# Hybrid attention block: the negated maximum of the softmax kept as a running minimum in the logits' reduction

## The chip, the cores and the metric

The kernel runs on one core of a Trainium2 chip. A core has five engines with queues of their own: TensorE (PE, matrix products), VectorE (DVE, elementwise work and reductions), ScalarE (ACT, functions), GpSimd (POOL) and SyncE (SP, which here issues nearly all DMAs). Each takes its instructions strictly in the order in which they stand in its queue and waits on semaphores for the others. The metric is the device time of one execution in microseconds (us), the median of three runs.

## The reference, cut to what matters

A decoder block over 2048 positions: a mix of sparse attention (8 heads of 64, one shared key and value) and a gated convolution, then cross attention and a feed-forward part. The change lies in the sparse attention. For each block of 128 queries an indexer picks 256 keys per query; the softmax runs over these alone:

```python
score = jnp.where(causal[None], score, -jnp.inf)
_, sel = lax.top_k(score, topk)
...
logits = jnp.einsum('bqhd,bqkd->bqhk', qb, k_sel).astype(jnp.float32) * (HEAD_DIM ** -0.5)
logits = jnp.where(valid[:, :, None, :], logits, -jnp.inf)
p = jax.nn.softmax(logits, axis=-1).astype(v.dtype)
return jnp.einsum('bqhk,bqkd->bqhd', p, v_sel)
```

## The kernel before

The kernel doesn't gather keys. It computes the logits of a block of queries against all keys up to its diagonal and adds a row of `bias` that is 0 for picked keys and -2^100 for the rest. There are 16 blocks. Block b has (b + 1) x 128 keys, cut into pieces of 512 (`cuts`, L794): blocks 0 to 3 have one piece, 4 to 7 two, 8 to 11 three, 12 to 15 four. `bg_attend` (L774) runs blocks 0 to 7 in one stretch and 8 to 15 in another much later; in both, other work is mixed in: projections and the output product on PE, the search for the 256th largest score on DVE and ACT, and a convolution of 31 taps on POOL (L941, a multiply L962 and an addition L963 per tap).

A block has four pairs of heads (hp). For each pair and piece, and each head e of the pair:

- L815, PE: two products give a tile of logits, 128 queries x up to 512 keys, in PSUM.
- L816, DVE: one instruction adds the bias, writes the masked logits to `prob` in SBUF, and puts their largest value into `mx[:, e, pi]`. The trace shows it as two, the reduction and a short read of the accumulator.
- L820 and L821, DVE, once per pair: the maximum over the pieces, then times -0.125, into `nm`. With one piece L823 alone does it.
- L840, ACT: exp(0.125 x logit + nm), in place, up to 1024 keys at a time, with the sum of each row.
- L889, PE: the probabilities are transposed, 128x128 at a time. L317 (ACT) writes the high part `pth`, L318 (DVE) the rest `ptl`; L854 and L855 (PE) multiply both with the values.
- L874 to L878: the output is transposed back, added up and multiplied by 1 / sum (L878, DVE) into `o`.

While a pair is transposed and multiplied, the logits of the next pair are computed ahead (L902 to L925). So DVE works in turn on the ptl of one pair and the logits of the next. The order on each engine's queue is written by a scheduler, which plays the program through with costs of its own: an instruction taken out or put in can move others.

Of the kernel before, what the change touches and what calls it, by code (L numbers as in the profile page):

```python
# [8 lines left out]
F32 = mybir.dt.float32  # L9
# [6 lines left out]
AF = mybir.ActivationFunctionType  # L16
ALU = mybir.AluOpType
AX = mybir.AxisListType
# [3 lines left out]
P = 128  # L22
# [39 lines left out]
def hybrid_block(ctx: ExitStack, tc: tile.TileContext, x, mem, positions, norm_mix_g, w_in, w_heads, w_out,  # L62
# [4 lines left out]
    V, G, S, PE = nc.vector, nc.gpsimd, nc.scalar, nc.tensor  # L67
# [25 lines left out]
    x, mem, out = x[0], mem[0], out[0]  # L93
# [193 lines left out]
    def right(name, bufs=2):  # L287
        return tc.tile_pool(name=name, bufs=bufs, side="right", reuse_waits="tile")
# [4 lines left out]
    def acc(shape, name="ps_acc"):  # L293
        return pp.tile(shape, F32, name=name, tag="acc", bufs=3)
# [479 lines left out]
    def bg_attend(blks, kv, deep, q0=None):  # L774
        with right("aq") as aq, right("at") as ap, right("av") as av:
# [4 lines left out]
            def block(b):  # L780
                if b not in per:
                    n = (b + 1) * P
                    bias = cb2[:, P - b * P:] if b < 2 else None
                    if bias is None:
                        bias = aq.tile([P, nmax], BF16, name="bias", tag="bias", bufs=ATB)
                        nc.sync.dma_start(out=bias[:, :n], in_=bias_d[b, :, :n])
                    qT = q0 if b == 0 else aq.tile([P, NH, P], F32R, name="qT", tag="qT", bufs=ATB)
                    if b:
                        load_r(qT, columns(q_d, slice(0, NH), b * P, P))
                    o = av.tile([P, NH, HD], F32, name="o", tag="o", bufs=ATB)  # L790
                    per[b] = bias, qT, o
                return per[b]

            def cuts(b):  # L794
                n = (b + 1) * P
                return [(p0, min(512, n - p0)) for p0 in range(0, n, 512)]

            def logits(b, hp, st):

                pcs = cuts(b)  # L800
                bias, qT, o = block(b)
                mx = aq.tile([P, 2, 4], F32, name="mx", tag="mx", bufs=4)
                st["nm"] = nm = aq.tile([P, 2], F32, name="nm", tag="nm")
                st["sm"] = aq.tile([P, 2, 4], F32, name="sm", tag="sm")
                st["pr"] = []
                for pi, (p0, w) in enumerate(pcs):
                    if p0 % 1024 == 0:
                        turn[0] += 1
                        st["pr"].append((ap, av)[turn[0] % 2].tile([P, 2, 1024], F32, name="prob", tag="prob",
                                                                   bufs=(PRA if nmax <= 1024 else PRB) // 2))  # L810
                    prob = st["pr"][-1][:, :, p0 % 1024:]
                    for e in range(2):
                        ps = acc([P, 512])
                        for a in range(2):
                            PE.matmul(ps[:, :w], qT[:, hp * 2 + e, :], ks[p0 // 512][:, a, :w], start=a == 0, stop=a == 1)  # L815
                        V.tensor_tensor_reduce(out=prob[:, e, :w], in0=ps[:, :w], in1=bias[:, p0:p0 + w], scale=1.0,  # L816
                                               scalar=-3.0e38, op0=ALU.add, op1=ALU.max, accum_out=mx[:, e, pi:pi + 1])
                        yield w
                if len(pcs) > 1:
                    V.tensor_reduce(out=nm, in_=mx[:, :, :len(pcs)], op=ALU.max, axis=AX.X)  # L820
                    V.tensor_scalar(out=nm, in0=nm, scalar1=-0.125, scalar2=None, op0=ALU.mult)  # L821
                else:
                    V.tensor_scalar(out=nm, in0=mx[:, :, 0], scalar1=-0.125, scalar2=None, op0=ALU.mult)  # L823

            last, turn = [None], [1]
            behind = []
# [6 lines left out]
            def exps(b, st, pi, es):  # L833

                w = min(1024, (b + 1) * P - pi * 1024)
                if w > 0:
                    for e in es:
                        pr = st["pr"][pi][:, e, :w]
                        with tc.issue_after(last[0]) if last[0] else nullcontext():
                            S.activation(out=pr, in_=pr, func=AF.Exp, scale=0.125, bias=st["nm"][:, e:e + 1],  # L840
                                         accum_out=st["sm"][:, e, pi:pi + 1])

            def weigh(b, hp, st):
# [59 lines left out]
            for _ in logits(*todo[0]):  # L903
                pass
            exps(todo[0][0], todo[0][2], 0, [0, 1])
            for cur, nxt in zip(todo, todo[1:] + [None]):
                ahead = logits(*nxt) if nxt else iter(())
# [977 lines left out]
    op = Scope(right("op"))  # L1885
    for half in range(2):
# [90 lines left out]
        op = Scope(right("op"))  # L1977
# [37 lines left out]
```

## Time and profile before

| | us |
|---|---|
| median of 3 runs | 3303.02 (3301.71 to 3306.49) |
| profiled execution | 3300.71, its span 3298.9 |
| PE busy | 3084.7 (94%) |
| DVE busy | 2478.3 (75%) |
| ACT busy | 1817.3 (55%) |
| POOL busy | 1337.0 (41%) |

The span runs from the first to the last instruction that the profiler saw; the execution's own time is a little longer. Busy shares are means over stages with different limits, so below they are taken by stretch. The first stretch of the sparse attention is about 436 to 760 us, the second about 1905 to 2262 us. In rows of the trace a line such as L816 names the line of the kernel, `out<-in` its tiles, and an arrow in brackets behind an idle time the instruction that ended it.

### The profile page before, as it was taken

Reading aid. Unit: us, or ns where it says so; the run is one execution under the profiler, and the core shown is the slowest. Engines: PE = TensorE matmul, PEld = TensorE weight load, DVE = VectorE, ACT = ScalarE, POOL = GpSimd, SP = SyncE. Lnnn points to the kernel's source line nnn. Section 1 sums busy time; section 2 is a strip of 40 time slices with the busy share of each in tenths; the row PEclk is TensorE's granted clock in tenths of the full one; section 3 lists DMA queues with packets and bytes.
Section 4 is the critical chain, followed back from the end, with each engine's and each line's share of the span. In section 5 each row is a group of like instructions: output and inputs, shape, how many; then the busy total and the mean of one; then the engine's idle time right before and its main releaser. Section 6 shows DMA issues by size and latency. Waiting matters only on the chain.

```text
span 3298.9 us, 45169 instructions
## 1 busy us (share of the span) xinstructions
PE 3084.7 (94%) x16162; PEld 2583.8 (78%) x16162; DVE 2478.3 (75%) x4964; ACT 1817.3 (55%) x3276; POOL 1337.0 (41%) x1141
## 2 busy tenths in 40 slices
PE   7987798999999998999999989999999999999998
PEld 5765576887877788788898878888878777777786
DVE  6899999877758688888788889986555766665445
ACT  6456466655458576667677667775443433333212
POOL 2999702999300699900000049991000144442000
PEclk9999899999999999999999989999999999999999
DMA  7452334543365312121222341103363322222432
GB/s 225 140 158 81 120 99 151 169 146 120 117 203 169 136 49 62 52 60 52 78 64 71 120 149 45 39 20 112 122 252 100 102 83 77 77 81 100 145 103 77
DMA packets 341960, 356.60 MB, mean 108 GB/s; under 512 B 21990, under 2 KB 268518, under 8 KB 340454
## 3 DMA queue, kind: packets, MB, share of 16 engines
q1 hardware_dynamic: 339302, 345.08, 32.8%
q0 software_dynamic: 2432, 8.64, 0.8%
q8 instruction: 127, 2.08, 0.3%
q14 instruction: 99, 0.81, 0.1%
HBM read 271.31 MB, written 82.34 MB: 107 GB/s over the span
## 4 chain that ended last, share of the span: by engine, by line
PE 55%; DVE 29%; ACT 9%; issue 5%; DMA 3%; SPq 0%; DVEq 0%; ACTq 0%
PE ps_w L1483 9%; PE ps_acc L277 6%; PE ps_acc L278 6%; PE ps_acc L276 6%; DVE jkc L687 4%; PE ps_s L277 4%; PE ps_s L278 4%; PE ps_s L276 4%; DVE wl L152 3%; PE ps_acc L815 3%; ACT junk L699 3%; DVE xa_cut L1515 2%; PE ps_tr L889 2%; PE ps_o L278 1%; PE ps_o L277 1%
## 5 line engine op out<-in xcount | busy, mean ns | idle before, releaser
L963 POOL TENSOR_TENSOR vt<-pr_c,vt 128x512 f32<-128x512 f32 x480 | 674.9, 1406 | 39.6
L152 DVE TENSOR_TENSOR wl<-raw,wh 128x1024 fp32r<-128x1024 f32 x252 | 335.2, 1331 | 220.8 <-ACT wh L147 216.1
L147 ACT ACTIVATE wh<-raw 128x1024 fp32r<-128x1024 f32 x252 | 264.8, 1051 | 368.9 <-PE ps_acc L278 174.4
L962 POOL TENSOR_SCALAR pr_c<-u,colsB 128x512 f32<-128x512 f32 x480 | 430.7, 897 | 45.1
L276 PE MATMUL ps_acc<-hp,wh 128*128 128x512 f32 x608 | 239.4, 395 | 0.9 <-ACT hp L322 0.7
L277 PE MATMUL ps_acc<-hp,wh 128*128 128x512 f32 x608 | 238.8, 393 | 0.0
L278 PE MATMUL ps_acc<-hp,wl 128*128 128x512 f32 x608 | 238.0, 392 | 0.0
L1256 POOL TENSOR_SCALAR xa<-xa,rs_y 128x1024 f32<-128x1024 f32 x4 | 4.4, 1123 | 498.6 <-DVE rs_y L170 498.6
L840 ACT ACTIVATE prob<-prob,nm 128x1024 f32<-128x1024 f32 (+7 forms) x192 | 172.1, 897 | 54.2 <-DVE nm L821 33.6
L815 PE MATMUL ps_acc<-kst,qT 128*128 128x512 f32 (+3 forms) x624 | 189.2, 395 | 9.7 <-DVE mx L816 5.1
L816 DVE CUSTOM_DVE_ANT_0 prob<-ps_acc,bias 128x512 f32<-128x512 f32 (+3 forms) x304 | 180.6, 615 | 15.1 <-PE ps_acc L815 12.7
L949 POOL DMA_DIRECT2D u<-u_d x16 | 9.3, 583 | 441.4 <-PE ps_tr L1187 228.4
L1458 POOL TENSOR_TENSOR hp_cut<-xb_cut 128x512 f32<-128x512 f32 x10 | 17.2, 1720 | 421.1 <-PE ps_tr L1404 364.6
L278 PE MATMUL ps_acc<-hh,wl 128*128 128x512 f32 (+1 forms) x384 | 157.8, 412 | 25.7 <-DVE wl L152 18.3
L317 ACT ACTIVATE pth<-ps_tr 128x512 fp32r<-128x512 f32 (+1 forms) x224 | 126.7, 574 | 94.5 <-PE ps_tr L889 84.0
L276 PE MATMUL ps_acc<-wh,hidh 128*128 128x256 f32 (+1 forms) x512 | 168.0, 328 | 7.8 <-ACT halo L1331 7.8
L1483 PE MATMUL ps_w<-T,wh 128*128 128x512 f32 x496 | 157.3, 399 | 18.0 <-DVE hp_cut L1494 18.0
L318 DVE TENSOR_TENSOR ptl<-ps_tr,pth 128x512 fp32r<-128x512 f32 (+1 forms) x224 | 145.7, 656 | 35.8 <-ACT pth L317 34.6
L276 PE MATMUL ps_acc<-hh,wh 128*128 128x512 f32 (+1 forms) x384 | 156.9, 415 | 15.6 <-ACT wh L147 14.7
L277 PE MATMUL ps_acc<-wl,hidh 128*128 128x256 f32 (+1 forms) x512 | 167.9, 328 | 0.0
L278 PE MATMUL ps_acc<-wh,hidl 128*128 128x256 f32 (+1 forms) x512 | 167.8, 328 | 0.0
L855 PE MATMUL ps_o<-ptl,vst 128*128 128x256 f32 x544 | 152.4, 302 | 12.2 <-DVE ptl L318 11.1
(481 smaller groups left out, 9894.9 us busy)
## 6 DMA issues: line engine op xcount, KB each, us to landing
raw<-in_w_down_dram SPq DMA_DIRECT2D x44, 512.0 KB
raw<-in_w_up_dram SPq DMA_DIRECT2D x34, 512.0 KB
raw<-in_w_gate_dram SPq DMA_DIRECT2D x34, 512.0 KB
raw<-in_w_out_dram SPq DMA_DIRECT2D x32, 512.0 KB
raw<-in_w_q_cross_dram SPq DMA_DIRECT2D x32, 512.0 KB
raw<-in_w_o_cross_dram SPq DMA_DIRECT2D x32, 512.0 KB
xt<-in_x_dram SPq DMA_DIRECT2D x24, 512.0 KB
raw<-in_w_in_dram SPq DMA_DIRECT2D x24, 512.0 KB
```

Source lines behind the costliest of these rows:

```text
L147: i = S.activation(out=hi, in_=src, func=AF.Copy)
L152: note(S=i, V=V.tensor_sub(out=lo, in0=src, in1=hi.bitcast(F32)))
L276: PE.matmul(ps, ah, bh, start=first, stop=False)
L277: PE.matmul(ps, ah, bl, start=False, stop=False)
L278: return PE.matmul(ps, al, bh, start=False, stop=last).ins
L815: PE.matmul(ps[:, :w], qT[:, hp * 2 + e, :], ks[p0 // 512][:, a, :w], start=a == 0, stop=a == 1)
L816: V.tensor_tensor_reduce(out=prob[:, e, :w], in0=ps[:, :w], in1=bias[:, p0:p0 + w], scale=1.0, scalar=-3.0e38, op0=ALU.add, op1=ALU.max, a ...
L840: S.activation(out=pr, in_=pr, func=AF.Exp, scale=0.125, bias=st["nm"][:, e:e + 1], accum_out=st["sm"][:, e, pi:pi + 1])
L855: PE.matmul(po, v, ptl[:, j - j0, :], start=False, stop=j == nst - 1)
L962: G.tensor_scalar(out=pr, in0=u[:, i:i + 512], scalar1=cb_w(i, c), scalar2=0.0, op0=ALU.mult, op1=ALU.add)
L963: G.tensor_add(out=vt[:, c, :], in0=pr, in1=vt[:, c, :])
L1483: PE.matmul(ps, x[:, k], y[:, k], start=first and k == i == 0, stop=k == 3 and i == 2, skip_group_check=True)
```

## The change

The reduction of L816 now also multiplies: it writes -0.125 times the masked logits and takes a minimum, which is the negated maximum that the exponential needs. From the second piece on it starts from the minimum of the pieces before (`mx[:, e, pi - 1:pi]`, a number per row in SBUF) instead of a constant, so that the last piece's result is the final one and is given to ACT as it is. L820, L821 and L823 are gone; the exponential's factor is -1; `mx` has six buffers instead of four, since ACT now reads it. Lines behind the change have numbers lower by 1 (L816 is L815) to 4 (L840 is L836).

```diff
--- before.py
+++ after.py
@@ -799,8 +799,7 @@
 
                 pcs = cuts(b)
                 bias, qT, o = block(b)
-                mx = aq.tile([P, 2, 4], F32, name="mx", tag="mx", bufs=4)
-                st["nm"] = nm = aq.tile([P, 2], F32, name="nm", tag="nm")
+                mx = aq.tile([P, 2, 4], F32, name="mx", tag="mx", bufs=6)
                 st["sm"] = aq.tile([P, 2, 4], F32, name="sm", tag="sm")
                 st["pr"] = []
                 for pi, (p0, w) in enumerate(pcs):
@@ -813,14 +812,11 @@
                         ps = acc([P, 512])
                         for a in range(2):
                             PE.matmul(ps[:, :w], qT[:, hp * 2 + e, :], ks[p0 // 512][:, a, :w], start=a == 0, stop=a == 1)
-                        V.tensor_tensor_reduce(out=prob[:, e, :w], in0=ps[:, :w], in1=bias[:, p0:p0 + w], scale=1.0,
-                                               scalar=-3.0e38, op0=ALU.add, op1=ALU.max, accum_out=mx[:, e, pi:pi + 1])
+                        V.tensor_tensor_reduce(out=prob[:, e, :w], in0=ps[:, :w], in1=bias[:, p0:p0 + w], scale=-0.125,
+                                               scalar=mx[:, e, pi - 1:pi] if pi else 3.0e38, op0=ALU.add, op1=ALU.min,
+                                               accum_out=mx[:, e, pi:pi + 1])
                         yield w
-                if len(pcs) > 1:
-                    V.tensor_reduce(out=nm, in_=mx[:, :, :len(pcs)], op=ALU.max, axis=AX.X)
-                    V.tensor_scalar(out=nm, in0=nm, scalar1=-0.125, scalar2=None, op0=ALU.mult)
-                else:
-                    V.tensor_scalar(out=nm, in0=mx[:, :, 0], scalar1=-0.125, scalar2=None, op0=ALU.mult)
+                st["nm"] = mx[:, :, len(pcs) - 1]
 
             last, turn = [None], [1]
             behind = []
@@ -837,7 +833,7 @@
                     for e in es:
                         pr = st["pr"][pi][:, e, :w]
                         with tc.issue_after(last[0]) if last[0] else nullcontext():
-                            S.activation(out=pr, in_=pr, func=AF.Exp, scale=0.125, bias=st["nm"][:, e:e + 1],
+                            S.activation(out=pr, in_=pr, func=AF.Exp, scale=-1.0, bias=st["nm"][:, e:e + 1],
                                          accum_out=st["sm"][:, e, pi:pi + 1])
 
             def weigh(b, hp, st):
```

The scheduler writes another order in both stretches. These are two places of the second one, in block 9 (pieces of 512, 512 and 256 keys) around the third pair of heads. On DVE, before: the last reduction of the pair (`mx_19372`), the product L878, then three ptl copies of the pair ahead with L820 and L821 between them, then the reductions of the next pair.

```order
L816 ISA prob_19411,mx_19372<-ps_acc_19416,bias_19136 128x256
L816 ISA mx_19372 128x1
L878 TENSOR_TENSOR o_19140<-o_19140,rr_19401 128x128
L318 TENSOR_TENSOR ptl_19427<-ps_tr_19421,pth_19426 128x512
L820 TENSOR_REDUCE nm_19373<-mx_19372 128x2
L318 TENSOR_TENSOR ptl_19443<-ps_s_19437,pth_19442 128x512
L821 TENSOR_SCALAR nm_19373<-nm_19373 128x2
L318 TENSOR_TENSOR ptl_19466<-ps_tr_19460,pth_19465 128x512
L816 ISA prob_19497,mx_19494<-ps_acc_19498,bias_19136 128x512
L816 ISA mx_19494 128x1
L816 ISA prob_19497,mx_19494<-ps_acc_19502,bias_19136 128x512
```

And now, the same pair (`mx_19274`), from its L878, which is L874 here:

```order
L874 TENSOR_TENSOR o_19048<-o_19048,rr_19302 128x128
L815 ISA prob_19312,mx_19274<-ps_acc_19313,bias_19044,mx_19274 128x256
L815 ISA mx_19274 128x1
L815 ISA prob_19312,mx_19274<-ps_acc_19317,bias_19044,mx_19274 128x256
L815 ISA mx_19274 128x1
L318 TENSOR_TENSOR ptl_19328<-ps_tr_19322,pth_19327 128x512
L318 TENSOR_TENSOR ptl_19342<-ps_s_19336,pth_19341 128x512
L318 TENSOR_TENSOR ptl_19365<-ps_tr_19359,pth_19364 128x512
L815 ISA prob_19395,mx_19393<-ps_acc_19396,bias_19044 128x512
L815 ISA mx_19393 128x1
L815 ISA prob_19395,mx_19393<-ps_acc_19400,bias_19044 128x512
```

The two small operations are gone from between the copies, both reductions of the last piece (256) now stand in front of the copies, and the reductions of the next pair alternate with copies. Those with a third source, `mx`, are the ones that start from memory.

On ACT, before: three copies (pth), then the exponentials of the same pair, which wait for `nm`.

```order
L317 ACTIVATE pth_19426<-ps_tr_19421 128x512
L317 ACTIVATE pth_19442<-ps_s_19437 128x512
L317 ACTIVATE pth_19465<-ps_tr_19460 128x512
L840 ACTIVATE prob_19375,sm_19374<-prob_19375,nm_19373 128x1024 x2
L858 ACTIVATE ot_19492<-ps_o_19430 128x256
L317 ACTIVATE pth_19480<-ps_tr_19475 128x512
L840 ACTIVATE prob_19411,sm_19374<-prob_19411,nm_19373 128x256
```

And now:

```order
L317 ACTIVATE pth_19327<-ps_tr_19322 128x512
L317 ACTIVATE pth_19341<-ps_s_19336 128x512
L317 ACTIVATE pth_19364<-ps_tr_19359 128x512
L836 ACTIVATE prob_19276,sm_19275<-prob_19276,mx_19274 128x1024 x2
L317 ACTIVATE pth_19379<-ps_tr_19374 128x512
L854 ACTIVATE ot_19391<-ps_o_19331 128x256
L836 ACTIVATE prob_19312,sm_19275<-prob_19312,mx_19274 128x256
```

The order of these is the same. The exponentials read `mx`, and each of the two waits for the reduction of its own head only.

## Rows read from the trace of the kernel before

**Rows 1.** Busy us (instructions) of PE, PEld, DVE, ACT, POOL by stretch; clock, DMA.
```profile
436.00:560.00 124.00, 107.91 (x568) 86.42 (x567) 118.09 (x419) 83.60 (x214) 8.40 (x10) 0.97 0.37 109
560.00:760.00 200.00, 184.30 (x1273) 163.83 (x1271) 158.38 (x330) 119.46 (x227) 186.02 (x162) 0.99 0.48 156
1905.00:2016.00 111.00, 98.51 (x606) 83.40 (x604) 100.39 (x284) 76.76 (x175) 69.94 (x66) 0.91 0.32 111
2016.00:2262.00 246.00, 241.98 (x1737) 215.72 (x1738) 218.91 (x598) 182.87 (x371) 204.61 (x205) 1.00 0.10 31
```

**Rows 2.** Chain of waits by line, second stretch, shares of its 357 us.
```profile
by line: PE ps_acc L815 19.6%; PE ps_tr L889 11.0%; PE ps_o L855 10.3%; DVE ptl L318 9.5%; PE ps_o L854 9.2%; PE ps_s L889 8.3%; DVE prob L816 5.3%; DVE nm L821 4.3%; ACT pth L317 3.3%; ACT prob L840 3.3%; issue 2.3%; DVE o L878 2.3%; PE ps
```

**Rows 3.** Groups of DVE instructions, second stretch: busy us, mean ns | idle before.
```profile
L816 DVE CUSTOM_DVE_ANT_0 prob<-ps_acc,bias 128x512 f32<-128x512 f32 (+3 forms) x224 | 135.0, 625 | 10.0 <-PE ps_acc L815 9.4
...
L821 DVE TENSOR_SCALAR nm<-nm 128x2 f32<-128x2 f32 x32 | 20.9, 652 | 0.0
...
L878 DVE TENSOR_TENSOR o<-o,rr 128x128 f32<-128x128 f32 x31 | 15.3, 494 | 0.1
...
L820 DVE TENSOR_REDUCE nm<-mx 128x2 f32<-128x6 f32 (+1 forms) x32 | 4.7, 148 | 0.0
```

**Rows 4.** Groups of DVE instructions, first stretch.
```profile
L821 DVE TENSOR_SCALAR nm<-nm 128x2 f32<-128x2 f32 x16 | 8.2, 513 | 0.3
...
L823 DVE TENSOR_SCALAR nm<-mx 128x2 f32<-128x2 f32 x16 | 2.6, 162 | 0.1
...
L820 DVE TENSOR_REDUCE nm<-mx 128x2 f32<-128x4 f32 x16 | 2.4, 149 | 0.1
```

**Rows 5.** Timeline of DVE: start us, us, line, operation, out<-in.
```profile
568.92 0.15 DVE L820 TENSOR_REDUCE nm<-mx 128x2 f32<-128x4 f32 x1
569.10 0.47 DVE L821 TENSOR_SCALAR nm<-nm 128x2 f32<-128x2 f32 x1
...
777.43 0.74 DVE L323 SCALAR_TENSOR_TENSOR hp<-ps_tr,colsA,hp 128x512 fp32r<-128x512 f32 x1
...
1955.94 6.28 DVE L821 TENSOR_SCALAR nm<-nm 128x2 f32<-128x2 f32 x1
...
1969.28 0.28 DVE L878 TENSOR_TENSOR o<-o,rr 128x128 f32<-128x128 f32 x1
...
1978.98 0.14 DVE L820 TENSOR_REDUCE nm<-mx 128x2 f32<-128x6 f32 x1
1979.05 0.68 DVE L318 TENSOR_TENSOR ptl<-ps_s,pth 128x512 fp32r<-128x512 f32 x1
1979.65 0.86 DVE L821 TENSOR_SCALAR nm<-nm 128x2 f32<-128x2 f32 x1
```

**Rows 6.** Timeline of POOL, the last row its last in the second stretch.
```profile
777.45 1.28 POOL L963 TENSOR_TENSOR vt<-pr_c,vt 128x512 f32<-128x512 f32 x1
...
1955.38 1.13 POOL L1256 TENSOR_SCALAR xb<-xb,rs_y 128x1024 f32<-128x1024 f32 x1
...
1979.19 1.29 POOL L963 TENSOR_TENSOR vt<-pr_c,vt 128x512 f32<-128x512 f32 x1
...
2237.11 1.28 POOL L963 TENSOR_TENSOR vt<-pr_c,vt 128x512 f32<-128x512 f32 x1
```

**Rows 7.** Timeline of PE: in brackets the idle time before, and its releaser.
```profile
1962.87 0.58 PE L855 MATMUL ps_o<-ptl,vst 128*128 128x256 f32 x1 [6.01 <-DVE ptl L318]
```

**Rows 8.** Timeline of ACT.
```profile
1980.54 1.15 ACT L840 ACTIVATE prob<-prob,nm 128x1024 f32<-128x1024 f32 x1 [1.38 <-DVE nm L821]
```

**Rows 9.** Instructions of line 816: ns min/median/max, first and last start.
```profile
L816 DVE CUSTOM_DVE_ANT_0 prob<-ps_acc,bias x304: 275/679/694, 472.7 to 2244.7; 128x512 f32<-128x512 f32 x112, 128x384 f32<-128x384 f32 x16, 128x128 f32<-128x128 f32 x12, 128x256 f32<-128x256 f32 x12
```

**Rows 10.** Groups of DVE by shape, whole span.
```profile
L323 DVE SCALAR_TENSOR_TENSOR hp<-ps_tr,colsA,hp 128x512 fp32r<-128x512 f32 x56 | 40.6, 747 | 21.2 <-ACT hp L322 20.6
...
L508 DVE SCALAR_TENSOR_TENSOR th_g<-th_g,ps_s 128x512 f32<-128x512 f32 x8 | 5.5, 684 | 3.0 <-PE ps_s L278 3.0
```

**Rows 11.** Instructions of line 977 in 2200 to 2330 us.
```profile
L977 PE MATMUL ps_tr<-ident,vt x16: 271/272/327, 2294.4 to 2297.3; 128*128 128x128 f32 x16
```

## The prediction

> **What bounds the kernel now.** The change touches one piece of code, the attention over selected keys, which runs in two stretches: blocks 0 to 7 from about 436 to 760 us, and blocks 8 to 15 from about 1905 to 2262 us. I first read how busy the engines are there [rows 1]. TensorE (PE) is the busiest over the whole, and in 2016 to 2262 us it is at 242 of 246 us. Elsewhere in these stretches it leaves time: 108 of 124 us at the start of the first, 99 of 111 us at the start of the second, and there VectorE (DVE) is the full one, 118 of 124 us and 100 of 111 us. So both stretches hang on DVE and PE together, and DVE is the one the change acts on.
>
> Then the chain of waits for the second stretch [rows 2]. Most of it is PE, but three DVE lines stand in it: the copy of the low part (ptl), the reduction that this change edits (prob), and `nm L821` with 4.3%, which is a product on 128x2 numbers. So small an operation should not be there at all.
>
> The groups of DVE instructions say why [rows 3, 4]. L821 has a mean of 652 ns in the second stretch and 513 in the first. L823, the same operation on as many elements, belongs to blocks 0 to 3, in a window in which GpSimd (POOL) works 8 of 124 us [rows 1], and takes 162 ns. The difference is a wait inside the instruction. The single rows show for what: at 1979.65 us L821 takes 0.86 us and ends with POOL's addition that had begun at 1979.19 and lasts 1.29 us [rows 5, 6]. At 1955.94 us it takes 6.28 us, until POOL's back-to-back operations from 1955.38 us are through. In that time PE waited 6.01 us for a ptl queued behind it [rows 7]; behind the instance at 1979.65 ACT's exponential waited 1.38 us [rows 8]. The reduce L820 has no such wait (148 and 149 ns in the mean), nor has L816, the large reduction in front of it: 304 instances, none above 694 ns [rows 9].
>
> [...]
>
> **What goes.** A DVE instruction begins some 0.08 us before the one ahead of it has ended, so a small one takes less of the queue than its duration: L820 at 1978.98 is followed by the next at 1979.05, 0.07 us [rows 5].
> - Second stretch, 32 pairs of heads: L821 is 20.9 us, of which 32 x 0.162 = 5.2 are its own and 15.7 are waits. Queue time gone: 15.7 + 32 x 0.07 = 17.9 us. L820: 32 x 0.07 = 2.2. Together 20.1 us.
> - First stretch: L821 is 8.2 us, 16 x 0.162 = 2.6 its own, 5.6 waits; gone 5.6 + 1.1 = 6.7. L820 1.1 (up to 2.9 where L821 follows at once, as at 568.92 and 569.10, 0.18 us apart). L823 16 x 0.07 = 1.1. Together 8.9 us.
>
> **What comes.** From the second piece of keys on, the reduction starts from a number in memory, `mx[pi-1]`, instead of a constant. Blocks 4 to 7 have one such piece, 8 to 11 two, 12 to 15 three; with 4 pairs and 2 heads per block that is 32 instructions in the first stretch and 64 + 96 = 160 in the second. The trace of before has no L816 of that kind. The nearest pair of rows is L323 against L508: both read PSUM and SBUF over 128x512, the first with its scalar from memory, the second with a constant, 747 against 684 ns [rows 10], so 63 ns. One bound is nothing, the other is 63 ns for each plus a wait on POOL (below). I take 63: 10.1 us in the second stretch and 2.0 in the first. Each of these also waits for a DVE semaphore, on a result two reductions back. Where an instruction needs the result of the one just ahead (569.10) it starts 0.11 us later than otherwise; here another reduction of 0.2 to 0.6 us lies between, so I take nothing, and 192 x 0.11 = 21 us as the bound. DVE's minimum instead of maximum, the factor -0.125 and ACT's factor -1 are constants in the same instructions: nothing. The six buffers of mx instead of four only loosen a wait.
>
> **What moves.** The scheduler writes a new order for all engines in the two stretches; outside them the order is the same. DVE's small pair vanishes from between the ptl copies, and both last reductions now stand ahead of them, so that the exponentials' operand is there when ACT has done its three copies. On SP some thirty DMAs move, all within the first stretch but one load of weights, by a few places; on POOL one convolution start swaps with its neighbours. I take nothing for these, with some 5 us either way as an estimate.
>
> **The sum.** By DVE's queue the second stretch gives 20.1 - 10.1 = 10.0 us. By the chain it gives 4.3% of 357 us = 15.4, less what the dearer reductions add on it: prob has 5.3% = 18.9 us there, 30 instructions of 0.625 us, of which 160 of 224 are of the new kind, 21 x 0.063 = 1.3; so 14 us. I take 11, nearer to the queue, since the chain finds other ways in a stretch where PE is at 98%. The first stretch gives 8.9 - 2.0 = 6.9 us by the queue, but its L821 belong to blocks 4 to 7, in the window in which DVE is busy for 158 of 200 us and PE for 184; I take 3. Of these 14 us I give one back: the product L878 stands near, reads two SBUF tiles, and will catch some of POOL's instructions that L821 met. That makes 13 us. The profiled execution took 3300.7 us (span 3298.9), 2.3 below the median, so 3287.7 there and 3290 against the median.
>
> What is late next: the convolution on POOL, which nobody hurries, ends its last block at 2238.4 us, and the PE transposes that need it come at 2294.4 [rows 6, 11]. That slack of 56 us covers the gain. After that PE is the bound again and passes the gain to the end.
>
> **Rivals.**
> - *No change to be measured.* PE at 242 of 246 us hides what DVE gains, and L878 takes over the waits for POOL. If all 21.3 us of waits move to it, DVE saves 29.0 - 21.3 = 7.7 and pays 12.1, plus 4.4 us: 3297 to 3307. For it: POOL works for 205 of 246 us there, and L878 comes as often as L821. Against it: the next L878 after the wait of 6.28 us is seven microseconds behind its end, at 1969.28 [rows 5], and POOL is through by then.
> - *Slower: the new scalar meets POOL.* If reading mx from memory makes a reduction wait for POOL as L821 does, 160 of them pay 15.7 / 32 = 0.49 us, 78 us of DVE queue in the second stretch against the 10 saved. DVE has 27 us free in its last 246, so some 41 us reach the end: 3344. From 0.06 us each on the gain of that stretch is gone. Against it: L323, with PSUM, SBUF and a scalar in SBUF, takes 0.74 us at 777.43 with POOL's addition running from 777.45 [rows 5, 6], and 747 as the mean. [...]
> - *Slower: the new order.* The order decides which tile of probabilities PE gets next; where PE is put in front of a ptl that isn't there yet it loses what L855 lost at 1962.87, and four such waits, 24 us, turn the gain of 13 into a loss of 11: 3314. Nothing in the rows excludes it, but the waits of before are mostly far shorter.
> - *More.* The exponentials' wait of 1.4 us per pair [rows 8] goes entirely and pulls the loop of reductions, exponentials and copies tight in the 12 pairs of blocks 9 to 11, where PE has room: 12 x 1 us on top of the forecast, 3278.
>
> **How the numbers follow.** A difference under 0.2%, 6.6 us, can't be told from none. Chances: the forecast 0.52 (its own range 3281 to 3296), more 0.16, no change 0.20, the new order 0.07, the scalar against POOL 0.05. Faster is the first two, 0.68; same 0.20; slower 0.12. The lower end is all 29.0 us gone and no price for the scalar, 3274, rounded to 3275; the upper the no-change case with its 4.4 us, 3307.
>
> **What would show it.** L820, L821 and L823 gone from DVE, 112 instructions fewer. L816 with a scalar at about 745 ns for 128x512, without one below 694; if the former is spread up to 1.5 us and more, the scalar meets POOL. The second stretch shorter by about 11 us and the first by 3, the rest as before. L878's mean above 494 ns would say that it took over waits. The forecast is wrong if both stretches keep their length, or if DVE's busy time falls and PE's idle time does not.

## The result and the profile after

The changed kernel takes 3288.3 us, the median of five runs (3278.3 to 3294.4); the kernel before took 3303.0 beside it. The ratio is 0.9949, with a 95% interval of 0.9934 to 0.9965: about 15 us faster, 1.7 us below the forecast of 3290. The profiled execution took 3288.3 us as well (span 3286.5).

First the stretches, cut as in [rows 1], by the changed kernel's own time:

```profile
436.00:560.00 124.00, 109.64 (x593) 87.92 (x592) 119.30 (x406) 86.05 (x222) 12.65 (x11) 0.99 0.40 118
560.00:760.00 200.00, 185.33 (x1287) 164.77 (x1286) 156.43 (x311) 123.70 (x234) 186.03 (x162) 1.00 0.49 158
1905.00:2016.00 111.00, 100.96 (x653) 86.00 (x651) 102.04 (x278) 81.53 (x189) 66.99 (x64) 0.94 0.32 111
2016.00:2262.00 246.00, 242.92 (x1775) 220.02 (x1775) 212.16 (x545) 177.26 (x357) 206.06 (x207) 1.00 0.14 44
```

PE gets more done in the same microseconds (568 to 593 instructions in the first row, 606 to 653 in the third, 1737 to 1775 in the last), and PE's granted clock is a little higher in three of the four (0.97, 0.99 and 0.91 before; 0.99, 1.00 and 0.94 now). In the last row DVE is busy for 212 us and not 219.

The chain of waits of the second stretch [rows 2] says who gave way. `nm L821` had 4.3% and is gone; the copy of the low part (ptl) falls from 9.5 to 3.0%, and the reduction, though each is dearer now, from 5.3 to 2.4%. What is left is nearly all PE:

```profile
by line: PE ps_acc L814 22.0%; PE ps_tr L885 13.5%; PE ps_o L851 12.9%; PE ps_o L850 11.9%; PE ps_s L885 9.4%; issue 3.5%; DVE ptl L318 3.0%; PE ps_s L276 2.9%; PE ps_s L277 2.9%; PE ps_s L278 2.8%; ACT prob L836 2.6%; DVE prob L815 2.4%; P
```

The queue of DVE itself, second stretch (line 815 is the old 816, 874 the old 878) [rows 3]:

```profile
L815 DVE CUSTOM_DVE_ANT_0 prob<-ps_acc,bias,mx 128x512 f32<-128x512 f32 (+3 forms) x160 | 103.0, 661 | 0.3 <-PE ps_acc L814 0.2
...
L815 DVE CUSTOM_DVE_ANT_0 prob<-ps_acc,bias 128x512 f32<-128x512 f32 x64 | 42.2, 686 | 7.9 <-PE ps_acc L814 7.2 <-PE ps_s L885 0.5
L874 DVE TENSOR_TENSOR o<-o,rr 128x128 f32<-128x128 f32 x32 | 22.0, 686 | 0.1
```

and the first stretch [rows 4]:

```profile
L874 DVE TENSOR_TENSOR o<-o,rr 128x128 f32<-128x128 f32 x31 | 16.8, 543 | 0.2
L815 DVE CUSTOM_DVE_ANT_0 prob<-ps_acc,bias,mx 128x128 f32<-128x128 f32 (+3 forms) x32 | 16.7, 543 | 2.5 <-PE ps_acc L814 2.4
```

Here is the first surprise. L820, L821 and L823 are gone, but the last product of each pair, L874, has grown from 15.3 to 22.0 us in the second stretch and from 14.1 to 16.8 in the first (one instance more falls into the second window, 0.3 us). One of its instances shows how. The changed kernel's timeline of DVE (start us, us):

```profile
1958.27 5.42 DVE L874 TENSOR_TENSOR o<-o,rr 128x128 f32<-128x128 f32 x1
```

POOL's at that time, equal neighbours drawn together (x2):

```profile
1956.72 2.22 POOL L1252 TENSOR_SCALAR xb<-xb,rs_y 128x1024 f32<-128x1024 f32 x2
1958.90 4.63 POOL L1253 TENSOR_TENSOR xb<-xb,gfin 128x1024 f32<-128x1024 f32 x2
```

And PE's, with the idle time before and its releaser in brackets:

```profile
1964.15 2.07 PE L814 MATMUL ps_acc<-kst,qT 128*128 128x512 f32 x4 [4.76 <-DVE mx L815]
```

The product starts at 1958.27, while POOL works at four operations without a gap (two of L1252, two of L1253), and ends 5.42 us later, 0.16 us after the last of them. PE then waits 4.76 us for a reduction queued behind it. Before, it was L821 that took 6.28 us against the same four operations [rows 5, 6], and PE waited 6.01 us for a ptl [rows 7].

The price of the scalar from memory, by shape over the whole span:

```profile
L815 DVE CUSTOM_DVE_ANT_0 prob<-ps_acc,bias,mx 128x512 f32<-128x512 f32 x120 | 87.5, 741 | 2.7 <-PE ps_acc L814 2.6
...
L815 DVE CUSTOM_DVE_ANT_0 prob<-ps_acc,bias 128x512 f32<-128x512 f32 x104 | 69.3, 685 | 10.4 <-PE ps_acc L814 9.2 <-PE ps_s L885 0.5 <-PE ps_tr L885 0.2
...
L815 DVE CUSTOM_DVE_ANT_0 prob<-ps_acc,bias,mx 128x128 f32<-128x128 f32 x24 | 7.6, 343 | 0.0
...
L815 DVE CUSTOM_DVE_ANT_0 prob<-ps_acc,cb 128x128 f32<-128x128 f32 x8 | 2.2, 287 | 1.8 <-PE ps_acc L814 1.8
```

741 against 685 ns for 512 columns and 343 against 287 for 128: 56 ns at both widths, where L323 and L508 had promised 63 [rows 10]. And the spread over all 192 (ns, min, median, max), to be set beside [rows 9]:

```profile
L815 DVE CUSTOM_DVE_ANT_0 prob<-ps_acc,bias,mx x192: 332/736/754, 553.0 to 2233.9; 128x512 f32<-128x512 f32 x120, 128x128 f32<-128x128 f32 x24, 128x256 f32<-128x256 f32 x24, 128x384 f32<-128x384 f32 x24
```

None is above 754 ns, though POOL was busy for 206 of the last 246 us: none of the 192 readings of mx shows a wait for POOL.

ACT's waits for the exponentials' operand in the second stretch (us in total, times, longest), in the kernel before:

```profile
ACT prob L840 <- DVE nm L821: 23.5, 18, 6.9
```

In the changed kernel:

```profile
ACT prob L836 <- DVE mx L815: 4.7, 1, 4.7
```

The 23.5 us over 18 pairs that L821 held up the exponentials are down to one wait of 4.7, that behind the product of 5.42 us.

Where along the span the time was won is read from three operations on PE that stand at the same place in both programs: the first transpose behind the first stretch, the first product of the second stretch, and the transpose that needs the last convolution (ns min/median/max, then first and last start). Before (the third is in [rows 11], 2294.4):

```profile
L1018 PE MATMUL ps_tr<-ident,xa x32: 272/273/477, 767.1 to 792.1; 128*128 128x128 f32 x32
...
L815 PE MATMUL ps_acc<-kst,qT x448: 219/393/796, 1907.1 to 2243.8; 128*128 128x512 f32 x122, 128*128 128x128 f32 x10, 128*128 128x256 f32 x9, 128*128 128x384 f32 x9
```

After:

```profile
L1014 PE MATMUL ps_tr<-ident,xa x32: 272/273/476, 757.3 to 782.7; 128*128 128x128 f32 x32
...
L814 PE MATMUL ps_acc<-kst,qT x448: 222/393/796, 1905.5 to 2232.9; 128*128 128x512 f32 x122, 128*128 128x128 f32 x10, 128*128 128x256 f32 x9, 128*128 128x384 f32 x9
...
L973 PE MATMUL ps_tr<-ident,vt x16: 270/273/327, 2283.5 to 2286.3; 128*128 128x128 f32 x16
```

The first stretch ends 9.8 us earlier (767.1 to 757.3), the second starts only 1.6 us earlier (1907.1 to 1905.5), and after it the lead is 10.9. So the second stretch gave 9.3 us, the first 9.8, and 8.2 were lost in between, in code that the change doesn't touch (run before_again below looks at that loss). POOL's last instruction of the convolution in the second stretch, in its timeline:

```profile
2238.75 1.28 POOL L959 TENSOR_TENSOR vt<-pr_c,vt 128x512 f32<-128x512 f32 x1
```

It ends at 2240.0, 43 us ahead of the transpose that needs it.

### The profile page after: what moved, and what is told of

The parts are those of the page before. It is cut to its first block, busy times and chain, and to the rows that moved or that the text cites. A ratio compares the mean times of both kernels' runs of the same rounds, so it can differ in the third digit from the quotient of the medians.

```text
span 3286.5 us, 45179 instructions
## 1 busy us (share of the span) xinstructions
PE 3073.2 (94%) x16162; PEld 2577.8 (78%) x16162; DVE 2464.3 (75%) x4852; ACT 1814.3 (55%) x3276; POOL 1339.2 (41%) x1141
## 4 chain that ended last, share of the span: by engine, by line
PE 53%; DVE 29%; ACT 9%; issue 5%; DMA 3%; SPq 0%; POOLq 0%; DVEq 0%; ACTq 0%
PE ps_w L1479 9%; PE ps_acc L276 6%; PE ps_acc L277 6%; PE ps_acc L278 6%; DVE jkc L687 5%; PE ps_s L277 4%; PE ps_s L278 4%; PE ps_s L276 4%; DVE wl L152 3%; ACT junk L699 3%; PE ps_acc L814 3%; DVE xa_cut L1511 2%; PE ps_tr L885 2%; DVE ca L1326 2%; PE ps_o L851 2%
## 5 line engine op out<-in xcount | busy, mean ns | idle before, releaser
L1252 POOL TENSOR_SCALAR xa<-xa,rs_y 128x1024 f32<-128x1024 f32 x4 | 4.4, 1124 | 504.5 <-DVE rs_y L170 504.5
L814 PE MATMUL ps_acc<-kst,qT 128*128 128x512 f32 (+3 forms) x624 | 180.5, 387 | 12.8 <-DVE mx L815 8.9
L836 ACT ACTIVATE prob<-prob,mx 128x1024 f32<-128x1024 f32 (+7 forms) x192 | 172.4, 899 | 27.5 <-DVE mx L815 27.1
L1479 PE MATMUL ps_w<-T,wh 128*128 128x512 f32 x496 | 157.3, 399 | 17.9 <-DVE hp_cut L1490 17.9
L850 PE MATMUL ps_o<-pth,vst 128*128 128x256 f32 x544 | 159.8, 311 | 1.3 <-ACT y_c L991 1.0
L277 PE MATMUL ps_acc<-hl,wh 128*128 128x512 f32 (+1 forms) x384 | 158.8, 414 | 0.0
```

The costliest lines, as they stand in the source:

```text
L277: PE.matmul(ps, ah, bl, start=False, stop=False)
L836: S.activation(out=pr, in_=pr, func=AF.Exp, scale=-1.0, bias=st["nm"][:, e:e + 1], accum_out=st["sm"][:, e, pi:pi + 1])
L850: PE.matmul(po, v, pth[:, j - j0, :], start=j == 0, stop=False)
L1479: PE.matmul(ps, x[:, k], y[:, k], start=first and k == i == 0, stop=k == 3 and i == 2, skip_group_check=True)
```

## The experiments

All ratios are to the kernel before, with their 95% intervals; 0.001 is 3.3 us. "The product" is the last one of a pair (L878 before, L874 after).

**The chain of scalars taken out, one small minimum back (run fold).**

```diff
-  scalar=mx[:, e, pi - 1:pi] if pi else 3.0e38,
+  scalar=3.0e38,
...
+  if len(pcs) > 1:
...
+      V.tensor_reduce(out=st["nm"], in_=mx[:, :, :len(pcs)], op=ALU.min, axis=AX.X)
```

> The change without its chained scalar: the minimum over minus eight stays, every reduction starts from a constant again, and one small minimum over the pieces (the former L820) stands behind the last of them; the product (L821, L823) stays away. Theory (L821's waits for POOL were the gain, the chained scalar a price of 56 ns each): 192 x 0.056 = 10.8 us leave DVE's queue against the changed kernel and 48 small reductions of 0.07 to 0.11 us come back, 3 to 5 us; DVE 6 us shorter, 3 to 6 us of it in the time: 3282 to 3286; the small reductions at 150 ns without a wait. Rival (the scalar's price is hidden, and the chain let the exponentials start earlier): 3290 to 3294, slower than the changed kernel's 3288. A third (any product of the operation L821 being gone is all that counts): 3288 as the changed kernel.

Measured: 3283.17 us, ratio 0.9930 (0.9917 to 0.9942), inside the first theory's numbers. The groups of the whole span:

```profile
L877 DVE TENSOR_TENSOR o<-o,rr 128x128 f32<-128x128 f32 x64 | 37.0, 578 | 0.3
...
L822 DVE TENSOR_REDUCE nm<-mx 128x2 f32<-128x4 f32 (+2 forms) x48 | 7.1, 147 | 0.2
```

The small minimum takes 147 ns, and the product waits about as much as in the changed kernel. That the scalar's price is what went is not shown by this alone: the interval touches that of the changed kernel, and run no_chain below speaks against it.

**The small operation put back (run small_back).**

```diff
-  st["nm"] = mx[:, :, len(pcs) - 1]
+  V.tensor_scalar(out=nm, in0=mx[:, :, len(pcs) - 1], scalar1=1.0, scalar2=None, op0=ALU.mult)
```

> The changed kernel with the small operation put back: behind the last reduction a 128x2 TENSOR_SCALAR (times one) copies the running minimum to nm, which the exponentials read; all else as changed. Theory (waiting for POOL in this operation is what was removed): it takes 0.5 to 0.65 us in the mean again, the product behind it falls back from 0.61 to about 0.47 us, and the time goes back by 10 to 18 us, to 3298 to 3306. Rival (the gain came from the chained minimum or from the new order of the instructions, with L821's waits only passed on): within 3 us of the changed kernel, 3285 to 3291.

Measured: 3304.83 us, ratio 0.9998 (0.9989 to 1.0007). The whole gain is gone, though the minimum is still chained. Groups of the whole span:

```profile
L875 DVE TENSOR_TENSOR o<-o,rr 128x128 f32<-128x128 f32 x64 | 32.9, 515 | 0.3
...
L820 DVE TENSOR_SCALAR nm<-mx 128x2 f32<-128x2 f32 x64 | 30.3, 473 | 0.2
```

The same 64 small operations in ns (min, median, max):

```profile
L820 DVE TENSOR_SCALAR nm<-mx x64: 149/184/6882, 441.7 to 2249.5; 128x2 f32<-128x2 f32 x64
```

And ACT's waits for nm in the second stretch:

```profile
ACT prob L837 <- DVE nm L820: 19.2, 16, 7.8
```

The 64 small operations take 473 ns in the mean, the product falls back to 515, and ACT waits 19.2 us for nm again. The time is the theory's and not the rival's (3285 to 3291); of the details, the mean came out a little below the 0.5 to 0.65 us expected (it is 599 ns in the second stretch), and the product fell back only half of the way to 0.47.

**The same, in a form that doesn't meet POOL (run small_reduce).**

```diff
+  V.tensor_reduce(out=nm, in_=mx[:, :, len(pcs) - 1:len(pcs)], op=ALU.min, axis=AX.X)
```

> As run small_back (a small operation behind the last reduction hands the running minimum on to nm, in all 64 pairs of heads), but the operation is a TENSOR_REDUCE over one element in place of the TENSOR_SCALAR: the form of L820, which has shown no wait for POOL. small_back gave the whole gain back, 16.5 us over the changed kernel. Theory A (the wait for POOL inside the TENSOR_SCALAR is what costs): 3289 to 3294, the small reduction at 150 ns. Theory B (any operation between the last reduction and the exponentials costs, by its latency and its place in DVE's queue, and the order that goes with it): 3297 to 3305.

Measured: 3287.46 us, ratio 0.9946 (0.9932 to 0.9960), the changed kernel's time, 1.5 us under theory A's lower end. All 64 small reductions, in ns (min, median, max):

```profile
L820 DVE TENSOR_REDUCE nm<-mx x64: 123/144/157, 442.1 to 2237.1; 128x2 f32<-128x2 f32 x64
```

The product, over the whole span:

```profile
L875 DVE TENSOR_TENSOR o<-o,rr 128x128 f32<-128x128 f32 x64 | 37.2, 581 | 0.3
```

Same 128x2 numbers, same operand for the exponentials, and nearly the same place: in 58 of the 64 pairs the small operation has the same neighbours on DVE as in small_back, and the two traces' orders agree for all but 94 of 4916 instructions of DVE and 149 of 16162 of PE. Only the operation differs, and with it the wait. So neither the operation's own time, nor its latency, nor the new order cost the 17 us (0.9998 against 0.9946), but the wait for POOL inside it, with what follows from that. The longest of the 64 reductions here takes 157 ns, the longest of small_back's 64 small operations 6.88 us.

**The product made to read PSUM, on the changed kernel and on the kernel before (runs after_psum, before_psum).**

```diff
-  V.tensor_add(out=op_, in0=ps[:, :, :HD], in1=op_)
-  (V, G)[0].tensor_mul(out=op_, in0=op_, in1=rr...)
+  V.tensor_add(out=ps[:, :, :HD], in0=ps[:, :, :HD], in1=op_)
+  (V, G)[0].tensor_mul(out=op_, in0=ps[:, :, :HD], in1=rr...)
```

> The changed kernel with the sum in front of the last product written to its PSUM tile, so that the product reads PSUM and SBUF and no longer two SBUF tiles. Theory (two SBUF inputs meet POOL, PSUM and SBUF don't): the product falls from 611 to about 280 ns in the mean with none above 350; 21 us leave DVE in all, the waits that it had taken over from L821 (about 9 us) among them; time 8 to 15 us below the changed kernel: 3273 to 3280. Rival 1 (the product waits whatever it reads, since it is the operation and not its place): mean stays near 600, 3288. Rival 2 (the waits are passed on to the next instruction with two SBUF inputs, or DVE has room behind the product): mean 280, but 3285 to 3291.

> The kernel before, with that same edit of the product alone (its two small operations on maxima stay). Theory: the product falls from 469 to about 280 ns, 12 us leave DVE, but L821 stands near it and catches part of what it met: L821's mean in the second stretch goes up from 652 to 700 ns or more, and 3 to 8 us reach the time: 3295 to 3300. Rival (no handing over between the two, gains add up): 10 to 13 us, 3290 to 3293, with L821's mean as it was. A third: no change, 3303.

Measured: after_psum 3273.95 us, ratio 0.9906 (0.9892 to 0.9919); before_psum 3292.71, ratio 0.9960 (0.9948 to 0.9973). The first is the fastest kernel of this study, 14.4 us below the changed one. Its product over the whole span, in ns (min, median, max):

```profile
L874 DVE TENSOR_TENSOR o<-ps_tr,rr x64: 271/284/292, 448.4 to 2240.4; 128x128 f32<-128x128 f32 x64
```

The groups of before_psum:

```profile
L821 DVE TENSOR_SCALAR nm<-nm 128x2 f32<-128x2 f32 x48 | 28.7, 598 | 0.3
...
L878 DVE TENSOR_TENSOR o<-ps_tr,rr 128x128 f32<-128x128 f32 x64 | 18.1, 283 | 0.3
```

From PSUM none of 64 products takes more than 292 ns, with POOL as busy as ever (207.7 us of the last 246 in after_psum, 206.1 in the changed kernel); from two SBUF tiles the longest was 5.42 us. In before_psum L821 does not take over what the product met: its mean is 598 ns, before 606, and in the second stretch 663 ns, before 652. The theory had said 700 or more there and 3295 to 3300; the rival, that the gain adds up in full (3290 to 3293), was right. The handing over goes one way in these runs: the product catches what L821 leaves, and L821 does not catch what the product leaves.

**Both edits together (run fold_psum).**

> Two edits together on the changed kernel: every reduction starts from a constant again with one small minimum behind the last (run fold), and the last product reads PSUM (run after_psum). Alone they took 5.1 and 14.4 us off the changed kernel's 3288.3. Theory (DVE's queue is still what the two stretches wait for): they add, 3267 to 3271. Rival (PE at 244 of 246 us takes no more): 3272 to 3276, as after_psum alone.

Measured: 3275.07 us, ratio 0.9911 (0.9896 to 0.9925), the rival's number. With the waits gone, the scalars' price doesn't show in the time; the intervals leave it some 5 us. The window of the last 246 us of the second stretch, in after_psum:

```profile
2016.00:2262.00 246.00, 244.19 (x1812) 223.88 (x1811) 203.02 (x529) 175.76 (x349) 207.69 (x208) 1.00 0.18 57
```

The same in fold_psum:

```profile
2016.00:2262.00 246.00, 243.51 (x1814) 222.90 (x1813) 201.55 (x548) 177.70 (x352) 204.19 (x204) 1.00 0.18 56
```

DVE has some 43 us free there in the first, PE 2.

**The chain left out without a substitute (run no_chain).**

```diff
-  scalar=mx[:, e, pi - 1:pi] if pi else 3.0e38,
+  scalar=0.0,
```

> The changed kernel with every reduction started from a constant, and nothing in place of the chain: the exponentials take the last piece's minimum (or zero where that is less), so the combination over the pieces is left out. It prices the scalar from memory alone, 192 x 56 ns = 10.8 us of DVE. Theory (DVE's queue holds back the stretches): 4 to 8 us below the changed kernel's 3288, a little below run fold's 3283 since 48 small reductions are gone too: 3279 to 3283. Rival (the price lies beside other work): 3286 to 3290.

Measured: 3287.56 us, ratio 0.9946 (0.9931 to 0.9961), the rival's number. 192 x 56 ns = 10.8 us less work on DVE moved the time by 0.0003, of which each interval leaves 0.0015 either way. The lower half of the theory's 4 to 8 us lies within that, so the run speaks for the rival without excluding a small price. The product took 38.4 us here and 39.1 in the changed kernel, so the waits were about the same.

**The change in one stretch at a time (runs only_late, only_early).**

```diff
+  new = b >= 8          (only_early: b < 8)
...
+  scale=-0.125 if new else 1.0, ..., op1=ALU.min if new else ALU.max
```

> The change in blocks 8 to 15 (the second stretch) alone; blocks 0 to 7 keep their maxima and small operations. In the profile of the changed kernel PE was 9.8 us ahead of the kernel before at the end of the first stretch, lost 8.1 of it until 1900 us, and won 9.2 in the second. Theory A (most of what the first stretch wins is given back on the way, by waits that return): this run keeps the second stretch's gain: 8 to 11 us below the kernel before, with only 3 to 6 us more for the whole change. Theory B (the loss on the way is chance, of one execution): 6 to 8 us below the kernel before, half of the whole change's gain.

> The change in blocks 0 to 7 (the first stretch) alone. With run only_late it should make up the whole change: that run took 10.4 us off the kernel before, the whole change 14.7 to 15.9. Theory (the stretches add): 4 to 6 us below the kernel before, 3297 to 3300. Rival (the first stretch's lead of 8 to 10 us in the profile reaches the end): 3293 to 3296. Waits for POOL between 560 and 765 us: as many as before, near 26 us, passed on to the product and to others.

Measured: only_late 3293.7 us, ratio 0.9968 (0.9958 to 0.9978), or 10.6 us; only_early 3295.25, ratio 0.9966 (0.9953 to 0.9979), or 11.2 us. Together 21.8 against the 16.8 of the whole change, each uncertain by 3 to 5: they add, within that. only_late lies in theory A's range, but the reason given there, waits that return on the way, is not shown (before_again below). only_early lies in its rival's: the first stretch alone gives more than the 3 us of the prediction and than the 4 to 6 expected here. The 26 us of waits expected between 560 and 765 us were not counted. The product over the whole span in only_late:

```profile
L884 DVE TENSOR_TENSOR o<-o,rr 128x128 f32<-128x128 f32 x64 | 37.6, 588 | 0.3
```

And in only_early:

```profile
L884 DVE TENSOR_TENSOR o<-o,rr 128x128 f32<-128x128 f32 x64 | 30.6, 478 | 0.3
```

It takes over waits where the small operations went: nearly all in the second stretch for only_late (37.6 us in place of 30.0), little for only_early (30.6).

**The kernel before once more (run before_again).**

> The kernel before, with nothing changed, for a second profile of it. Seven profiled kernels lost 1 to 8 us between 760 and 1900 us against the first profiled execution of the kernel before, in code that none of them edits. If that execution was a quick one there by chance, this one loses 2 to 5 us on it as well; if the loss belongs to the edits (whatever wins in the first stretch gives it back), it stays within 1 us. Time 3300 to 3306.

Measured: 3306.73 us, ratio 1.0005 (0.9991 to 1.0019). Its three places on PE:

```profile
L1018 PE MATMUL ps_tr<-ident,xa x32: 272/273/473, 767.6 to 792.6; 128*128 128x128 f32 x32
...
L815 PE MATMUL ps_acc<-kst,qT x448: 223/393/796, 1911.7 to 2249.0; 128*128 128x512 f32 x122, 128*128 128x128 f32 x10, 128*128 128x256 f32 x9, 128*128 128x384 f32 x9
...
L977 PE MATMUL ps_tr<-ident,vt x16: 271/273/327, 2299.6 to 2302.5; 128*128 128x128 f32 x16
```

From the first to the second place it takes 1911.7 - 767.6 = 1144.1 us, where the first execution took 1140.0 and the changed kernel 1148.2. So half of the 8.2 us that seemed lost there is chance of the first profile of before. In the other profiled kernels with the full convolution this part took 1140.7 to 1145.5 us. What stays is at most 4 us, no more than executions differ by.

**A quiet POOL (runs before_quiet, after_quiet).**

```diff
-  if onpool:
+  if onpool and i > 2:
+      pass
+  elif onpool:
```

> The kernel before with a quiet POOL: of the 31 taps of the convolution that POOL works out, all but the first three are left out (so part of the computation is missing; its time is only compared with that of the changed kernel with the same cut). L821 takes about 162 ns in both stretches, as L823 does, and L878 about 280. How far the time falls below 3303 is open; 20 to 80 us, since other VectorE lines meet POOL too.

> The changed kernel with that same cut of the convolution's taps. Theory (the gain is L821's waits for POOL, the rest about cancels): with POOL quiet the change takes 48 x 0.07 + 48 x 0.07 to 0.11 + 16 x 0.07 = 8 to 10 us off DVE's queue and adds 192 x 0.056 = 10.8: no change against the kernel before with the same cut, within 4 us. Rival (the new order or the earlier exponentials made the gain): 8 to 16 us faster than that kernel.

Measured: before_quiet 3171.89 us, after_quiet 3163.03, so by the medians the change still gives 8.9 us (0.28%), where the theory allowed 4 and the rival began at 8. The ratios, 0.9597 (0.9581 to 0.9613) and 0.9575 (0.9558 to 0.9592), put it at 7.3 us, and their intervals overlap; in the two profiled executions the first stretch ended only 1.2 us earlier and the second was 0.5 us shorter. The pair thus decides neither way. The expectation that L821 would take 162 ns was wrong too. Groups of before_quiet:

```profile
L878 DVE TENSOR_TENSOR o<-o,rr 128x128 f32<-128x128 f32 x64 | 20.6, 322 | 0.3
...
L821 DVE TENSOR_SCALAR nm<-nm 128x2 f32<-128x2 f32 x48 | 16.2, 337 | 0.3
```

Its longest L821, in the timeline of DVE:

```profile
1837.08 6.30 DVE L821 TENSOR_SCALAR nm<-nm 128x2 f32<-128x2 f32 x1
```

The product of after_quiet:

```profile
L874 DVE TENSOR_TENSOR o<-o,rr 128x128 f32<-128x128 f32 x64 | 24.6, 384 | 0.3
```

POOL's four operations on xb are not part of the convolution; that L821 meets them here as well is taken from its length, 6.30 us against 6.28 before. L821 keeps 16.2 - 48 x 0.162 = 8.4 us of waits; with the product's, 20.6 - 64 x 0.28 = 2.7 us, that is 11.1, of which the changed kernel has 24.6 - 64 x 0.28 = 6.7 left. 4.4 us of the 8.9 are waits; the other half is not settled, and the run is no clean test of what it was meant to test. The cut itself takes 132 us off the kernel before, where 20 to 80 were expected; where from was not followed up.

**The runs with the full convolution on one line.** Length of the second stretch (from the first product to the transpose behind it, as above) against the waits of its small operations (busy time less 162 ns each) and of its products (less 280 ns each), worked out from the groups of each trace:

| run | small ops | products | waits, us | stretch, us |
|---|---|---|---|---|
| before_again | 15.9 | 7.0 | 22.9 | 387.9 |
| before | 15.7 | 6.6 | 22.3 | 387.3 |
| only_early | 15.5 | 6.2 | 21.7 | 384.0 |
| small_back | 14.0 | 7.7 | 21.7 | 383.5 |
| before_psum | 16.0 | 0.2 | 16.2 | 380.7 |
| no_chain | 0 | 15.7 | 15.7 | 377.3 |
| only_late | 0 | 15.1 | 15.1 | 378.9 |
| after | 0 | 13.0 | 13.0 | 378.0 |
| fold | 0 | 12.7 | 12.7 | 373.8 |
| small_reduce | 0 | 12.6 | 12.6 | 375.9 |
| after_psum | 0 | 0.2 | 0.2 | 367.9 |
| fold_psum | 0 | 0.2 | 0.2 | 364.6 |

The length is about 364 us plus the waits, one for one, to within 4 us. The scalars' 160 x 56 ns = 9 us show at most in part: at about the same waits the stretch is 4.2 us shorter without them in fold than in after, 3.3 in fold_psum than in after_psum, and 0.7 in no_chain than in after, at 2.7 us more of waits. These are single executions, and the differences are no larger than the table's scatter.

## Why the prediction came out right, and which of its terms did not

- *What bounds, and what L821 was.* Right. The time hung on DVE's queue in front of PE, and on L821's wait for POOL: small_back brings it back and the gain is gone, small_reduce brings the operation back without the wait and the gain stays.
- *What goes, 20.1 and 8.9 us.* Of it the waits, 15.7 and 5.6, are what counted. The 7.7 us of queue time that the small operations take themselves (17.9 - 15.7 + 2.2 in the second stretch, 8.9 - 5.6 in the first) don't show: small_reduce puts 64 small operations back into the queue and stands at the changed kernel's time.
- *What comes, 10.1 and 2.0 us.* The size was about right (56 ns for 63), the place was not. The prediction's sum by the queue put the whole price there as a loss. Taking it away gained 6 us (fold, 0.0019), 1 us (no_chain, 0.0003) and nothing (fold_psum against after_psum, 0.0005 the other way), each uncertain by some 5 to 7 us: most of the price lies beside DVE's other work, and whether a few us of it reach the end is open. The self-wait costs nothing, as taken: DVE is idle for 0.3 us ahead of the 160 reductions with a scalar.
- *One microsecond given back to the product.* This step was mis-sized worst. By the groups of the whole span, L878 had 30.0 - 64 x 0.28 = 12.1 us of waits and L874 has 39.1 - 17.9 = 21.2: it took over 9.1 of L821's 21.3. The argument against, that the next product after the 6.28 us stands seven microseconds behind, fails since the program shifts against POOL: in the changed kernel a product starts at 1958.27, within the row of POOL's operations that L821 had met. No run shows the one microsecond, and two SBUF tiles were only its stated reason; the runs show 9.1 us handed over, and none of 64 products above 292 ns once one of the two inputs is in PSUM (after_psum).
- *The sum.* The queue's sum had 12.1 us for a scalar that cost little or nothing, 8 too few for what the product took over, and 7.7 us of queue time as gain that no run shows: errors of opposite sign. The 11 us then taken between queue and chain, and the 3 for the first stretch, were judgements and not sums. So the mechanism was right, and that the time came within 2 us is partly luck. Counted afterwards, the waits alone give 33.4 us before, 21.2 after, 12.2 gone, against 14.7 by the medians (16.8 by the ratio). The error in the split shows as well: -11 and -3 by stretch were 9.3 and 9.8 in the profile, and about equal in only_late and only_early.
- *Late next.* As said: the convolution on POOL ends at 2240.0 us and is needed at 2283.5, still 43 us apart.
- *Rivals.* "No change" had the right mechanism, the product taking over, and too much of it: 43% of the waits, not all. "The scalar meets POOL" is out, by the 754 ns. "The new order" was not tried by itself, but small_back has a new order too, and it stands at the time of the kernel before and 17 us above small_reduce, whose order is nearly the same; the table's scatter of some 4 us holds what an order does. "More" did not come: ACT's waits for the exponentials' operand fell by 18.8 us, but the time stands 10 us above the 3278 of that rival, and small_reduce, where ACT waits for the operand again (10.7 us over 13 pairs), is no slower.
- *The clock.* Neither the sum nor the table has this term. By the clocks of [rows 1] and of the rows after, PE lost 0.03 x 124 + 0.01 x 200 + 0.09 x 111 = 15.7 us of full-speed time in the stretches before, and 0.01 x 124 + 0.06 x 111 = 7.9 after. The difference of 7.8 us is an upper estimate of what the clock gave, out of the 19.1 us of the two profiles; it holds if PE was the limit all the while, and the clocks are rounded. It doesn't decide alone: small_back has the higher 0.94 as well and no gain. How much of it the waits caused and how much is chance is not shown.
- *What stays open.* Why the first stretch gives 6 us (the whole change less only_late) to 11 (only_early) where its own waits fell by 5.6 - (16.8 - 14.1) = 2.9 only, and the unexplained half of the quiet pair's 8.9 us, which may be the same thing; the clock, 0.97 and 0.99 in the first stretch before and 0.99 and 1.00 after, may hold part of it. ACT waits less for the exponentials' operand there (22.4 us against 28.9), but small_reduce, where it waits 26.9 us, lost nothing in the timed runs.

## What to carry to other kernels

An instruction on 128x2 numbers that took 0.6 us in the mean here was not small work but a wait, and the same form at a quiet time (162 ns) shows how much of it. Before taking such a one away, ask which neighbour will stand in its place: of the waits it had, 43% (9.1 of 21.3 us) went to the product that met POOL next. Changing the form took the wait away at its root in these runs: a reduction for a product with a number (157 ns the longest of 64, against 6.88 us), PSUM for one of two SBUF inputs (292 ns the longest of 64, against 5.42 us). Two edited lines on the product gave 13 us without the change and 14 on top of it.

## What the runs showed of the hardware that was not expected

How small a thing can wait how long. The prediction had read L821's 6.28 us from 1955.94 as a wait for a row of POOL's instructions; the runs show it again in the changed kernel, with the product, and in small_back. POOL's timeline in the kernel before, equal neighbours drawn together:

```profile
1955.38 2.21 POOL L1256 TENSOR_SCALAR xb<-xb,rs_y 128x1024 f32<-128x1024 f32 x2
1957.56 4.63 POOL L1257 TENSOR_TENSOR xb<-xb,gfin 128x1024 f32<-128x1024 f32 x2
```

Four instructions follow one another from 1955.38 to 1962.19, and L821, of 128x2 numbers, ends at 1962.22, behind the fourth. In small_back one of 6.88 us does the same: it starts at 1963.57, 0.04 us ahead of the first of POOL's four, and ends at 1970.45, 0.03 us behind the fourth. So in these two, as for the changed kernel's product of 5.42 us, the wait ended with the last of POOL's back-to-back instructions and not with the first.

Such a wait can cost PE more than its own length. After the 6.01 us of [rows 7] PE works on at a granted clock of 0.52 in the mean of 7 us. These 7 us, from 1962 on, in the kernel before:

```profile
1962.00:1969.00 7.00, 6.13 (x26) 5.79 (x27) 5.37 (x18) 4.87 (x12) 1.28 (x3) 0.52 0.66 225
```

The same in small_reduce, where PE had no such wait (its longest in the second stretch was 2.5 us):

```profile
1962.00:1969.00 7.00, 6.81 (x49) 5.67 (x48) 6.71 (x19) 5.95 (x13) 4.78 (x4) 1.00 0.29 68
```

At the clock of 0.52 stand 26 matrix products, of mixed sizes, in the time in which the other kernel does 49 at 1.00. That is another 7 x 0.48 = 3.4 us of full-speed time, an estimate from these clocks. The changed kernel has the same behind its 4.76 us (0.56 in these 7 us), since its product takes over this longest wait nearly whole. That the wait brought the lower clock is read from these three windows; no run tests it.

A scalar from memory in place of a constant costs the reduction 56 ns at 128 columns (343 against 287) and at 512 (741 against 685), so between these widths it is a cost per instruction and not per element.
